# A two-layer SSD, GLA and attention trunk on one core: packed first loads, an earlier norm root, value products beside the next scores, and a rewritten tail

## The chip, the cores and the metric

The kernel runs on one core of a Trainium2 chip. The time is the device time of one execution, in microseconds (us). A core has five engines with a queue of instructions each: PE (TensorE, matrix products; PEld stands for its weight loads), DVE (VectorE), ACT (ScalarE), POOL (GpSimd) and SP (SyncE, which here only starts transfers). Transfers between memory and the core are started from the queue of SP or of ACT.

## What is computed

Sequence 256, width 1024, one batch, fp32. Layer one projects the normed input once and runs an SSD branch (causal convolution, 16 heads) and a GLA branch (8 heads) on parts of it; layer two is an attention whose block is as long as the sequence, so that only the own block, a causal softmax, remains:

```python
def ssd_gla_layer(x, norm_w, w_in, ...):
    h = rms_norm(x, norm_w)
    u = h @ w_in
    z_a, xbc, dt_raw, q_b, k_b, v_b, gate_lr, g_b = split_cols(u, EVEN_SPLITS)
    xbc = silu(causal_depthwise_conv(xbc, conv_w, conv_b))
    y_a = rms_norm(ssd_chunked_scan(...) * silu(z_a), ssd_norm_w)
    log_decay = log_sigmoid(gate_lr @ gate_w2 + gate_b) / 16
    o_b = rms_norm(gla_chunked(q_b, k_b, v_b, log_decay), gla_norm_w) * silu(g_b)
    return x + concatenate([y_a, o_b]) @ w_out

def moba_layer(x, norm_w, w_in, w_out):
    q, k, v, z = split(rms_norm(x, norm_w) @ w_in, 4)   # 16 heads of 64
    o = moba_attention(q, k, v)                         # one block of 256: causal softmax
    return x + (o * silu(z)) @ w_out

reference = lambda x: rms_norm(moba_layer(ssd_gla_layer(x)), final_norm)
```

## The kernel before

Every large product is made in three: both factors are split into a high part (ACT copies, L76) and a low part (DVE subtracts, L77), and PE adds high times high, low times high and high times low (`mm` at L159). In names, `r_` is a raw weight tile, `h_` its high and `l_` its low part. Weights come in chunks over SP's queue (`fetch`, L70) into four buffers, in the order of a list of pieces (`plan`), and are split some chunks ahead (`prefetch`).

PE runs its instructions in exactly the order in which the code writes them. A small model clock decides while the program is written: each product adds its modelled time (`spend`), and steps of coroutines whose delay (table `DL`) is over are written in between the products of the main loop (`spawn`, `step`, `due`). On the other engines a scheduler places the work, but for the first stage, where DVE and ACT too stand in written order.

The stages that the change touches:

- Start. Twenty warm-up products of a zero tile (`warmp`, L177, count `NWARM`). The transposed input `xT` comes in eight chunks (kb) of 128 rows over SP's queue, each followed by the weights of both first column chunks (`a01`, 2 x 416 columns); the constants `cst`, with the norm weights `en` among them, come over ACT's queue (L184). For each chunk the input is scaled by `en` and split (`hh`, L216 to L219), the weights are split (`h_a`, `l_a`), and PE makes twelve products into four banks `pa` (`gemm_a01`). The norm itself is taken out of the products: squares of x are summed to `xsq` (ACT by pairs of chunks at L223, DVE adds), PE sums over rows (`ss`, ahead of chunk 7's products), DVE and POOL make `rcol`, the inverse root (L232, L233), and `tm_evac` scales the banks out with it: `dtr`, `glr` on DVE and `v` on ACT (L266). The next product group, `pb`, takes the first bank that comes free.
- Main list. `ORDER_A` gives the order of column blocks of the input projection: numbers are blocks of 128 columns (convolution input, GLA's queries and keys 14 to 17), "a2" to "a4" are 416-column chunks (value and gate). `GLA_NEEDS` says which of these each GLA part waits for. A block is 24 products, `ks` (L547) is GLA's scaled key.
- Attention. Four groups g of two pairs of heads. For each group the main loop writes the projections `pp` (queries and keys, then gates z), and the coroutine `co_attn` writes scores `as`, the softmax (row maximum as a negated `nm` on DVE at L773, exponent on ACT at L775), transposes `ptp`, and value products `ao` into a bank of the pool `psm`; `og` is ao times the gate, split into `oghi`, `oglo`.
- Tail. The last projection `pf` is made row block by row block (tt = 0, 1); `add_res` adds the residual (L841) and lets ACT sum the squares (L843), `scale_w` multiplies by the final norm's weight `fnb` (L846), `finish` makes the inverse root (L850, L851), scales both halves (ACT L854, DVE L856) and stores them over ACT's and SP's queues. The last 256 columns of tt = 1 have a bank of their own, `pflast`.

## Time and profile before

| what | value |
|---|---|
| device time, median of 3 runs (lowest, highest) | 340.99 us (340.92, 341.36) |
| profiled execution, its own time | 340.65 us |
| its span, first to last instruction | 338.9 us |
| mean granted PE clock | 0.993 |
| busy: PE, PEld, DVE, ACT, POOL | 98%, 87%, 76%, 69%, 9% |
| moved by DMA | 56.06 MB, mean 165 GB/s |

The profile is of one execution. The 1.75 us between its time and its span lie ahead of the first and behind the last instruction. A row of a timeline gives the start, the busy time of a run of like instructions, the engine, the line of code, the operation, output and inputs, their count, and in brackets how long the engine had been idle and what released it. Matmuls overlap in PE's pipeline, so a row's busy time is longer than the step from one product to the next.

### The profile page before, as it was taken

What the parts mean: (1) busy time and instruction counts of PE and PEld (TensorE: products, weight loads), DVE (VectorE), ACT (ScalarE), POOL (GpSimd) and SP (SyncE); (2) the same over time, 40 slices, a digit from 0 to 9 for tenths busy, and PEclk for the clock granted to TensorE, in tenths of its full rate; (3) what the DMA queues carried; (4) which work ended last, traced back from release to release, by engine and by line L of the source; (5) the groups of instructions that cost most, each with busy time, mean ns of one, the idle gap of its engine ahead of it and who ended that gap; (6) DMA issues with size and microseconds to landing.
All of it is one profiled execution on the core that took longest, in us unless ns stands there. A gap on an engine that the chain in (4) does not pass through costs nothing.

```text
span 338.9 us, 5921 instructions
## 1 busy us (share of the span) xinstructions
PE 331.0 (98%) x2160; PEld 295.0 (87%) x2160; DVE 257.1 (76%) x535; ACT 234.8 (69%) x499; POOL 29.7 (9%) x42
## 2 busy tenths in 40 slices
PE   8999999999999999999999999999999999999992
PEld 8999989999899899999888888888888888888791
DVE  3978978999997569789974775467869698696552
ACT  4958699899675758677452676475696887978541
POOL 1000010002100141434210000000000000000000
PEclk9999999999999999999999999999999999999997
DMA  7996784462377454431685635757507346070002
GB/s 227 340 329 198 233 233 134 135 203 91 97 211 263 143 156 158 161 127 55 203 294 192 200 119 179 248 150 240 170 17 254 105 142 232 1 248 3 0 20 106
DMA packets 18093, 56.06 MB, mean 165 GB/s; under 512 B 2048, under 2 KB 5120, under 8 KB 17936
## 3 DMA queue, kind: packets, MB, share of 16 engines
q1 hardware_dynamic: 17344, 53.53, 49.1%
q10 hardware_dynamic: 720, 2.16, 1.8%
q8 instruction: 17, 0.28, 0.3%
q14 instruction: 12, 0.10, 0.1%
HBM read 54.63 MB, written 1.05 MB: 164 GB/s over the span
## 4 chain that ended last, share of the span: by engine, by line
PE 96%; issue 2%; DVE 1%; ACT 0%; POOLq 0%; POOL 0%
PE pb L159 22%; PE pp L159 20%; PE pa L159 14%; PE pc L159 13%; PE pv L159 6%; PE pf L159 5%; PE yp L159 2%; PE ao L159 2%; PE go L159 2%; PE as L159 2%; PE gs L159 2%; PE ptp L163 2%; PE warmp L177 1%; PE obt L163 1%; PE lg L159 1%
## 5 line engine op out<-in xcount | busy, mean ns | idle before, releaser
L159 PE MATMUL pb<-hh,h_b 128*128 128x256 f32 x416 | 76.9, 286 | 0.0
L159 PE MATMUL pp<-h,h_p 128*128 128x512 f32 x192 | 67.7, 403 | 0.0
L159 PEld LDWEIGHTS pb<-hh,h_b 128*128 128x128 f32 x416 | 64.7, 191 | 1.4 <-issue 0.9
L159 PE MATMUL pb<-hh,l_b 128*128 128x256 f32 x208 | 58.8, 282 | 0.0
L159 PE MATMUL pp<-h,l_p 128*128 128x256 f32 x192 | 49.9, 280 | 0.0
L159 PE MATMUL pa<-h_a,hh 128*128 128x416 f32 x160 | 42.9, 360 | 0.0
L159 PEld LDWEIGHTS pp<-h,h_p 128*128 128x128 f32 x192 | 34.5, 188 | 7.0 <-issue 0.5
L159 PEld LDWEIGHTS pb<-hh,l_b 128*128 128x128 f32 x208 | 39.8, 191 | 0.0
L159 PEld LDWEIGHTS pp<-h,l_p 128*128 128x128 f32 x192 | 36.2, 189 | 2.2
L77 DVE TENSOR_TENSOR l_p<-r_p,h_p 128x1024 fp32r<-128x1024 f32 x24 | 29.2, 1223 | 9.2 <-ACT h_p L76 8.3
L77 DVE TENSOR_TENSOR l_b<-r_b,h_b 128x1024 fp32r<-128x1024 f32 x26 | 31.5, 1213 | 3.8 <-ACT h_b L76 3.8
L76 ACT ACTIVATE h_b<-r_b 128x1024 fp32r<-128x1024 f32 x26 | 27.2, 1062 | 9.3 <-DMA r_b<-in_wb 7.0
L159 PEld LDWEIGHTS pa<-h_a,hh 128*128 128x128 f32 x160 | 30.2, 191 | 1.3 <-issue 0.9
L76 ACT ACTIVATE h_p<-r_p 128x1024 fp32r<-128x1024 f32 x24 | 25.2, 1057 | 1.9 <-PE pv L159 1.6
L159 PE MATMUL pa<-l_a,hh 128*128 128x416 f32 x80 | 24.8, 351 | 0.0
L76 ACT ACTIVATE h_c<-r_c 128x1024 fp32r<-128x1024 f32 x16 | 16.9, 1055 | 10.2 <-DMA r_c<-in_wc 7.0
L77 DVE TENSOR_TENSOR l_c<-r_c,h_c 128x1024 fp32r<-128x1024 f32 x16 | 19.9, 1251 | 4.9 <-ACT h_c L76 4.9
L77 DVE TENSOR_TENSOR l_a<-r_a,h_a 128x832 fp32r<-128x832 f32 (+1 forms) x21 | 20.4, 978 | 2.3 <-ACT h_a L76 2.2
L76 ACT ACTIVATE h_a<-r_a 128x832 fp32r<-128x832 f32 (+1 forms) x21 | 18.0, 861 | 4.3 <-DMA r_a<-in_wa 3.1
L159 PE MATMUL pv<-h_v,h 128*128 128x512 f32 x64 | 20.2, 391 | 0.0
L775 ACT ACTIVATE pt<-pt,nm 128x128 f32<-128x128 f32 (+1 forms) x32 | 14.2, 443 | 5.6 <-DVE nm L773 5.6
L446 DVE SCALAR_TENSOR_TENSOR cu<-pad,cwh,cu 128x256 f32<-128x256 f32 x30 | 14.4, 481 | 1.3 <-ACT cu L444 1.2
(235 smaller groups left out, 700.9 us busy)
## 6 DMA issues: line engine op xcount, KB each, us to landing
r_b<-in_wb SPq DMA_DIRECT2D x26, 512.0 KB, 4.4
r_p<-in_wp SPq DMA_DIRECT2D x24, 512.0 KB, 4.2
r_c<-in_wc SPq DMA_DIRECT2D x16, 512.0 KB, 3.9
...
```

The costliest lines, as they stand in the source:

```text
L76: S.activation(hi, raw, AF.Copy)
L77: V.tensor_sub(lo, raw, hi.bitcast(F32))
L159: TE.matmul(out, lhsT, rhs, start=start, stop=stop)
L163: TE.transpose(out, in_, ident)
L177: TE.matmul(wps[:, 0:T], warm[:, 0:P], warm, start=True, stop=True)
L446: V.scalar_tensor_tensor(u, pd[:, 1 + i:1 + i + T], w(i), u, op0=ALU.mult, op1=ALU.add)
L775: S.activation(pt[:, cs], pt[:, cs], AF.Exp, scale=-1.0, bias=nm[:, tt:tt + 1], accum_out=sme[:, tt:tt + 1])
```

## The change

- Loads. A chunk of x^T, its column of norm weights and both weight chunks are packed in one array `xw`, 1092 columns per chunk (559 KB), loaded into shared buffers of the pool `big` and no longer into the four raw buffers. Chunks 0 and 1 come in two transfers: columns 0 to 676 (norm column, x, first weights, 346 KB) over SP's queue and the rest (213 KB) over ACT's; chunk 3 comes over ACT's queue, the others over SP's. `cst` follows on SP's queue. Chunks 6 and 7 use the buffers of 0 and 1 again.
- Fifteen warm-up products for twenty.
- The squares are made chunk by chunk; `ss` and the root `rcol` are written in the middle of chunk 6 and get high priority, as do `rsq` and the evacuation of the four banks. Two small operations on constants move to chunk 5.
- `ORDER_A`: "a3" stands between blocks 2 and 3 (it stood behind block 6), and some blocks behind it change places.
- Value products: for groups 0 to 2 the code of `ao` and `og` is put in a closure `last`, which the next group's coroutine calls ahead of its scores; its bank comes from the pool `psg`. Group 3 runs it behind its transposes. The loop that waited for z is gone.
- Tail: for tt = 1 DVE sums the squares, each sum going on from the last one and starting at D x EPS; `fnb` is multiplied by the root of D once; the root on POOL follows the last sum directly, at high priority; ACT scales and stores columns 0 to 384 and DVE 384 to 1024 (before: halves of 512).

```diff
-NWARM = 20
+XW = 4 + T + 2 * 416
+NWARM = 15
...
-ORDER_A = (8, 9, 10, 11, 0, 14, 1, 12, 2, 13, 3, 15, 5, 16, 4, 17, 6, "a3", 7, "a2", "a4")
+ORDER_A = (8, 9, 10, 11, 0, 14, 1, 12, 2, "a3", 3, 13, 5, 15, 4, 16, 6, 17, 7, "a2", "a4")
...
-    nc.scalar.dma_start(cst, cst_d)
...
+    xTs, ens = [], []
     for kb in range(KB):
-        nc.sync.dma_start(xT[:, kb, :], xT_d[:, kb, :])
-        load(1 if kb else 2)
+        raw = big.tile([P, XW], F32, name=f"xw{kb}", tag=("xT", "y", "gs", "obhi", "oblo", "v", "xT", "y")[kb])
+        for i, (c0, c1) in enumerate(((0, 676), (676, XW)) if kb < 2 else ((0, XW),)):
+            (nc.scalar if i or kb == 3 else nc.sync).dma_start(raw[:, c0:c1], xw_d[:, kb, c0:c1])
+        w = raw[:, 260:XW].rearrange("p (c n) -> p c n", c=2)
+        raws.extend([w[:, 0:1, :], w[:, 1:2, :]] if kb < 2 else [w])
+        ens.append(raw[:, 0:1])
+        xTs.append(raw[:, 4:260])
+    nc.sync.dma_start(cst, cst_d)
...
-    xsq = big.tile([P, KB, T], F32, name="xsq", tag="y")
+    xsq = tmp.tile([P, T], F32, name="xsq0", tag="t1g")
+    cwh = cpool.tile([P, 50], F32, name="cwh")
+    ea = cpool.tile([P, 16], F32, name="ea")
 
     with tc.manual_schedule(engines={mybir.EngineType.DVE, mybir.EngineType.Activation}):
         for kb in range(KB):
-            en = cst[:, C_EN + kb:C_EN + kb + 1]
+            en, xk = ens[kb], xTs[kb]
             if kb == 0:
-                V.tensor_scalar(hhi[:, kb, :], xT[:, kb, :], en, None, op0=ALU.mult)
+                V.tensor_scalar(hhi[:, kb, :], xk, en, None, op0=ALU.mult)
             else:
-                S.activation(hhi[:, kb, :], xT[:, kb, :], AF.Copy, scale=en)
-            V.scalar_tensor_tensor(hlo[:, kb, :], xT[:, kb, :], en, hhi[:, kb, :].bitcast(F32),
+                S.activation(hhi[:, kb, :], xk, AF.Copy, scale=en)
+            V.scalar_tensor_tensor(hlo[:, kb, :], xk, en, hhi[:, kb, :].bitcast(F32),
                                    op0=ALU.mult, op1=ALU.subtract)
-            prefetch(kb + 2)
-            if kb % 2:
-                S.activation(xsq[:, kb - 1:kb + 1, :], xT[:, kb - 1:kb + 1, :], AF.Square)
-                if kb > 1:
-                    V.tensor_tensor(xsq[:, 0:2, :], xsq[:, 0:2, :], xsq[:, kb - 1:kb + 1, :], op=ALU.add)
-        V.tensor_tensor(xsq[:, 0, :], xsq[:, 0, :], xsq[:, 1, :], op=ALU.add)
-        prefetch(10)
+            prefetch((2, 4)[kb] if kb < 2 else kb + 3)
+            sq = tmp.tile([P, T], F32, name=f"xsq{kb}", tag="t1f") if kb else xsq
+            S.activation(sq, xk, AF.Square)
+            if kb:
+                V.tensor_tensor(xsq, xsq, sq, op=ALU.add)
+            if kb == 5:
+                V.tensor_scalar(cwh, cst[:, C_CW:C_CW + 50], 0.5, None, op0=ALU.mult)
+                S.activation(ea, cst[:, C_AL:C_AL + 16], AF.Exp)
+        prefetch(11)
...
-            if kb == 0:
-                w = [tuple(a[:, 0, :] for a in need(("a01", 0, c))) for c in range(2)]
+            if kb < 2:
+                w = [tuple(a[:, 0, :] for a in need(("a01", kb, c))) for c in range(2)]
             else:
-                hi, lo = need(("a01", kb))
+                hi, lo = need(("a01", kb, 0))
                 w = [(hi[:, c, :], lo[:, c, :]) for c in range(2)]
             ts = [slice(tt * P, tt * P + P) for tt in range(2)]
             steps = [[(b, hhi[:, kb, ts[b[1]]], w[b[0]][0]), (b, hlo[:, kb, ts[b[1]]], w[b[0]][0]),
                       (b, hhi[:, kb, ts[b[1]]], w[b[0]][1])] for b in banks]
-            if kb == 0:
+            if kb < 2:
                 order = [t for h in (steps[0:2], steps[2:4]) for q_ in zip(*h) for t in q_]
             elif kb < KB - 1:
                 order = [t for q_ in zip(*steps) for t in q_]
             else:
-                env["rcol"] = rms_from_sum(colsum(xsq[:, 0, :], "ss1")[:, 0:2], 2, D, "rcol")
                 order = [t for q_ in steps for t in q_]
             seen = {}
-            for b, l_, r_ in order:
+            for n, (b, l_, r_) in enumerate(order):
+                if kb == KB - 2 and n == 6:
+                    with tc.high_priority():
+                        env["rcol"] = rms_from_sum(colsum(xsq, "ss1")[:, 0:2], 2, D, "rcol")
                 seen[b] = i = seen.get(b, -1) + 1
                 mm(ps[b][:, 0:416], l_, r_, kb == 0 and i == 0, kb == KB - 1 and i == 2)
...
+        with tc.high_priority():
+            V.tensor_tensor(rsq, rcol, rcol, op=ALU.mult)
+            for c in range(2):
+                for tt in range(2):
+                    tm_evac(c, tt, ps[c][tt])
...
+        if "ao" in env:
+            env.pop("ao")()
...
+            if pr == prs[0]:
+                yield DL["at1"]
+        def last():
+            ops = pg(f"ao{g}")
+            for n, pr in enumerate(prs):
+                hc = [slice(64 * (2 * pr + j), 64 * (2 * pr + j) + 64) for j in range(2)]
+                for j, r in enumerate(rows):
+                    mm(ops[r, n * T:n * T + T], va[:, 0, hc[j]], pTs[pr, j][:, 0:T], True, False)
+                for j, r in enumerate(rows):
+                    mm(ops[r, n * T + P:n * T + T], va[:, 1, hc[j]], pTs[pr, j][:, T:3 * P], False, True)
+            for n, pr in enumerate(prs):
+                og = tmp.tile([P, T], F32, name=f"og{pr}", tag="t1f")
+                V.tensor_tensor(og, ops[:, n * T:n * T + T], env[("z", pr)], op=ALU.mult)
+                S.activation(oghi[:, pr, :], og, AF.Copy)
+                V.tensor_sub(oglo[:, pr, :], og, oghi[:, pr, :].bitcast(F32))
+        if g < 3:
+            env["ao"] = last
+        else:
+            yield DL["at3"]
+            last()
...
+        if tt == 0:
+            S.activation(jk[:, 0:c1 - c0], x1[:, tt, cs], AF.Square, accum_out=ssf[:, tt, i:i + 1])
+        else:
+            V.tensor_tensor_reduce(out=jk[:, 0:c1 - c0], in0=x1[:, tt, cs], in1=x1[:, tt, cs], scale=1.0,
+                                   scalar=ssf[:, tt, i - 1:i] if i else D * EPS, op0=ALU.mult, op1=ALU.add,
+                                   accum_out=ssf[:, tt, i:i + 1])
...
+    V.tensor_scalar(fnb, fnb, D ** 0.5, None, op0=ALU.mult)
+    def root(tt, s):
+        rv = sm.tile([P, 1], F32, name=f"rv{tt}", tag="rv")
+        G.tensor_tensor(rv, s, mhalf[:, 0:1], op=ALU.pow)
+        return rv
+    def finish(tt, r):
         o = big.tile([P, D], F32, name=f"o{tt}", tag=f"s{tt}")
-        S.activation(o[:, 0:512], x1[:, tt, 0:512], AF.Copy, scale=r)
-        nc.scalar.dma_start(out_d[tt * P:tt * P + P, 0:512], o[:, 0:512])
-        V.tensor_scalar(o[:, 512:D], x1[:, tt, 512:D], r, None, op0=ALU.mult)
-        nc.sync.dma_start(out_d[tt * P:tt * P + P, 512:D], o[:, 512:D])
+        c = 384
+        S.activation(o[:, 0:c], x1[:, tt, 0:c], AF.Copy, scale=r)
+        nc.scalar.dma_start(out_d[tt * P:tt * P + P, 0:c], o[:, 0:c])
+        V.tensor_scalar(o[:, c:D], x1[:, tt, c:D], r, None, op0=ALU.mult)
+        nc.sync.dma_start(out_d[tt * P:tt * P + P, c:D], o[:, c:D])
...
+            if i == 1:
+                r = root(1, ssf[:, 1, 2:3])
         scale_w(512 + 256 * i, 768 + 256 * i, 1)
-        if i == 0:
-            V.tensor_tensor(sf[:, 1:2], ssf[:, 1, 0:1], ssf[:, 1, 1:2], op=ALU.add)
-            V.tensor_scalar(sf[:, 1:2], sf[:, 1:2], 1.0 / D, EPS, op0=ALU.mult, op1=ALU.add)
-    finish(1, sf[:, 1:2], ssf[:, 1, 2:3])
+    finish(1, r)
```

SP's queue at the start. Before, the list begins with:

```order
L190 DMA xT<-in_xT 128x256
L70 DMA r_a_0_0_113<-in_wa 128x416
L70 DMA r_a_0_1_115<-in_wa 128x416
L190 DMA xT<-in_xT 128x256
L70 DMA r_a_1_118<-in_wa 128x2x416
L190 DMA xT<-in_xT 128x256
L70 DMA r_a_2_121<-in_wa 128x2x416
```

The same queue after:

```order
L194 DMA xw_105<-in_xw 128x676
L194 DMA xw_108<-in_xw 128x676
L194 DMA xw_111<-in_xw 128x1092
L194 DMA xw_115<-in_xw 128x1092
L194 DMA xw_117<-in_xw 128x1092
L194 DMA xw_119<-in_xw 128x1092
L194 DMA xw_121<-in_xw 128x1092
L199 DMA cst<-in_cst 128x111
```

Seventeen transfers of x and weights became seven here and three on ACT's queue, and `cst` came over from ACT's queue to the end.

PE in the attention layer, where the value products of group 2 stand (`pp_1`, `pp_2` are projections of group 3, `as` its scores). Before:

```order
L159 MATMUL pp_1_3614<-h_2307,h_p_3496 128x512
L159 MATMUL pp_1_3614<-h_2307,l_p_3497 128x256
L159 MATMUL ao_3623<-pT_3535,va 64x256 x2
L159 MATMUL ao_3623<-pT_3535,va 64x128 x2
L159 MATMUL ao_3623<-pT_3586,va 64x256 x2
L159 MATMUL ao_3623<-pT_3586,va 64x128 x2
L159 MATMUL pp_1_3614<-h_2307,h_p_3496 128x512
L159 MATMUL pp_1_3614<-h_2307,l_p_3497 128x256
```

After:

```order
L159 MATMUL pp_2_3681<-h_2311,h_p_3573 128x512
L159 MATMUL pp_2_3681<-h_2311,l_p_3574 128x256
L159 MATMUL ao_3686<-pT_3539,va 64x256 x2
L159 MATMUL ao_3686<-pT_3539,va 64x128 x2
L159 MATMUL ao_3686<-pT_3590,va 64x256 x2
L159 MATMUL ao_3686<-pT_3590,va 64x128 x2
L159 MATMUL as_0_3703<-qk_1_3565,pp_0_s 128x128
L159 MATMUL as_1_3705<-qk_1_3565,pp_0_s 128x128
```

The value products moved from between key projections to directly ahead of the scores of group 3, some thirty rows further on.

DVE at the end, from the last-but-one addition of the residual on. Before:

```order
L841 TENSOR_TENSOR x_1662<-x_1662,pf_1_3782 128x256
L846 TENSOR_TENSOR x_1662<-x_1662,fnb 128x256
L885 TENSOR_TENSOR sf<-ssf 128x1
L886 TENSOR_SCALAR sf<-sf 128x1
L841 TENSOR_TENSOR x_1662<-x_1662,pflast 128x256
L846 TENSOR_TENSOR x_1662<-x_1662,fnb 128x256
L850 TENSOR_SCALAR rv_4005<-ssf,sf 128x1
L856 TENSOR_SCALAR o_4008<-x_1662,rv_4005 128x512
```

After (`ISA` is the reducing operation and the read of its sum):

```order
L862 TENSOR_TENSOR x_1666<-x_1666,pf_1_3787 128x256
L867 ISA jf_3976,ssf<-x_1666,ssf 128x256
L867 ISA ssf 128x1
L872 TENSOR_TENSOR x_1666<-x_1666,fnb 128x256
L862 TENSOR_TENSOR x_1666<-x_1666,pflast 128x256
L867 ISA jf_4004,ssf<-x_1666,ssf 128x256
L867 ISA ssf 128x1
L872 TENSOR_TENSOR x_1666<-x_1666,fnb 128x256
L888 TENSOR_SCALAR o_4009<-x_1666,rv_4006 128x640
```

The sums of squares came to DVE, its small additions went, and the last scaling grew from 512 to 640 columns.

## Rows read from the trace of the kernel before

**Rows 1.** Page, busy times; windows view of the tail: PE, PEld, DVE, ACT, POOL, clock.
```profile
PE 331.0 (98%) x2160; PEld 295.0 (87%) x2160; DVE 257.1 (76%) x535; ACT 234.8 (69%) x499; POOL 29.7 (9%) x42
...
325.20:338.90 13.70, 7.08 (x54) 6.64 (x53) 6.38 (x16) 4.01 (x12) 1.10 (x2) 0.83 0.20 78
```

**Rows 2.** Timeline of the first microseconds: start, busy us, engine, line, operation.
```profile
1.25 4.34 PEld L177 LDWEIGHTS warmp<-warm 128*128 128x128 f32 x20 [1.25 <-DVE mhalf L203]
...
4.42 1.11 ACT L76 ACTIVATE h_a<-r_a 128x416 fp32r<-128x416 f32 x2 [0.24 <-DMA r_a<-in_wa]
...
5.69 1.36 PE L159 MATMUL pa<-h_a,hh 128*128 128x416 f32 x4
...
7.27 0.91 PE L159 MATMUL pa<-h_a,hh 128*128 128x416 f32 x4
```

**Rows 3.** Timeline of PE alone from 6.3 on.
```profile
6.04 1.01 PE L159 MATMUL pa<-h_a,hh 128*128 128x416 f32 x3
```

**Rows 4.** Windows of the loading; last columns: granted clock, DMA share, GB/s.
```profile
2.00:3.00 1.00, 1.00 (x7) 1.00 (x6) 0.00 (x0) 0.53 (x1) 0.13 (x4) 1.00 0.79 173
3.00:4.00 1.00, 1.00 (x7) 1.00 (x7) 0.03 (x1) 0.03 (x1) 0.00 (x0) 1.00 0.99 347
```

**Rows 5.** Tile r_a in the first 20 us: durations ns min/median/max, first and last start.
```profile
L76 ACT ACTIVATE h_a<-r_a x9: 550/883/902, 4.4 to 17.1; 128x832 fp32r<-128x832 f32 x7, 128x416 fp32r<-128x416 f32 x2
L77 DVE TENSOR_TENSOR l_a<-r_a,h_a x9: 591/1018/1026, 5.0 to 18.1; 128x832 fp32r<-128x832 f32 x7, 128x416 fp32r<-128x416 f32 x2
```

**Rows 6.** Timeline around the first root.
```profile
21.98 0.50 PE L159 MATMUL ss<-ones,xsq 128*128 128x1 f32 x4
...
22.76 0.70 POOL L233 TENSOR_TENSOR rcol<-rcol_v,mhalf 128x2 f32<-128x2 f32 x1 [20.63 <-DVE rcol_v L232]
...
24.24 1.55 ACT L266 ACTIVATE v<-pa,rsq 128x384 f32<-128x384 f32 x3 [1.19 <-DVE glr L263]
...
24.52 0.34 PE L159 MATMUL pa<-l_a,hh 128*128 128x416 f32 x1
24.88 0.30 PEld L159 LDWEIGHTS pb<-hh,h_b 128*128 128x128 f32 x2 [0.35 <-ACT v L266]
```

**Rows 7.** Timeline of PE at the value products of group 2.
```profile
274.98 0.40 PE L159 MATMUL pp<-h,h_p 128*128 128x512 f32 x1
275.22 0.28 PE L159 MATMUL pp<-h,l_p 128*128 128x256 f32 x1
275.43 1.52 PE L159 MATMUL ao<-pT,va 128*64 128x256 f32 x16
276.88 0.50 PE L159 MATMUL pp<-h,h_p 128*128 128x512 f32 x1
277.21 0.28 PE L159 MATMUL pp<-h,l_p 128*128 128x256 f32 x1
```

**Rows 8.** Timeline at the start of group 3's softmax.
```profile
285.10 0.48 DVE L773 CUSTOM_DVE_ANT_0 pt<-as,mat,rq 128x256 f32<-128x256 f32 x1
285.27 0.40 ACT L775 ACTIVATE pt<-pt,nm 128x128 f32<-128x128 f32 x1 [1.38 <-DVE nm L773]
```

**Rows 9.** Timeline of GLA's scaled key on POOL and its first products.
```profile
84.66 1.21 POOL L547 COPY ks<-e 128x256 f32<-128x256 f32 x1 [3.52 <-DVE e L538]
...
111.67 0.37 PE L159 MATMUL gs<-qs,ks 64*128 64x128 f32 x1
```

**Rows 10.** Timeline of the tail.
```profile
332.32 0.42 DVE L841 TENSOR_TENSOR x<-x,pflast 128x256 f32<-128x256 f32 x1 [1.19 <-PE pflast L159]
...
333.94 0.55 POOL L851 TENSOR_TENSOR rv<-rv,mhalf 128x1 f32<-128x1 f32 x1 [5.33 <-DVE rv L850]
334.53 0.72 ACT L854 ACTIVATE o<-x,rv 128x512 f32<-128x512 f32 x1 [1.25 <-POOL rv L851]
...
335.05 0.34 SPq L857 DMA_DIRECT2D out<-o  x1
335.28 0.35 ACTq L855 DMA_DIRECT2D out<-o  x1
```

More of the change, by code (lines that the diff above doesn't have):

```diff
@@ L101, in plan_tm @@
             plan((name, q_), src[:, 2 * q_:2 * q_ + 2, :], 2, src.shape[2])
[L103 to L106 removed]
+    for kb in range(KB):
+        for c in range(2 if kb < 2 else 1):
+            plan(("a01", kb, c), None, 1 if kb < 2 else 2, 416)
     for j in ORDER_A:
         if isinstance(j, str):
[L109 removed]
+            plan_tm(j, wa_d[int(j[1]) - 2])
         else:
@@ L361, in co_first @@
         rcol = env["rcol"]
+        with tc.high_priority():
[3 more added lines that the diff above has]
+                    tm_evac(c, tt, ps[c][tt])
         V.tensor_scalar(rhalf, rcol, 0.5, None, op0=ALU.mult)
-        V.tensor_tensor(rsq, rcol, rcol, op=ALU.mult)
         V.tensor_scalar(rsv, rsq, 1.0 / P, None, op0=ALU.mult)
         V.tensor_scalar(rsh, rsq, 0.5, None, op0=ALU.mult)
-        V.tensor_scalar(cwh, cst[:, C_CW:C_CW + 50], 0.5, None, op0=ALU.mult)
-        S.activation(ea, cst[:, C_AL:C_AL + 16], AF.Exp)
-        for c in range(2):
-            for tt in range(2):
-                tm_evac(c, tt, ps[c][tt])
         env["a1"] = True
@@ L788, in co_attn @@
                 S.activation(pTs[pr, j], tp[:, 0:3 * P], AF.Copy)
-            yield DL["at1"] if pr == prs[0] else DL["at3"]
-        ops = pm(f"ao{g}")
-        for n, pr in enumerate(prs):
-            hc = [slice(64 * (2 * pr + j), 64 * (2 * pr + j) + 64) for j in range(2)]
-            for j, r in enumerate(rows):
-                mm(ops[r, n * T:n * T + T], va[:, 0, hc[j]], pTs[pr, j][:, 0:T], True, False)
-            for j, r in enumerate(rows):
-                mm(ops[r, n * T + P:n * T + T], va[:, 1, hc[j]], pTs[pr, j][:, T:3 * P], False, True)
-        while ("z", prs[1]) not in env:
-            yield 300
-        for n, pr in enumerate(prs):
-            og = tmp.tile([P, T], F32, name=f"og{pr}", tag="t1f")
-            V.tensor_tensor(og, ops[:, n * T:n * T + T], env[("z", pr)], op=ALU.mult)
-            S.activation(oghi[:, pr, :], og, AF.Copy)
-            V.tensor_sub(oglo[:, pr, :], og, oghi[:, pr, :].bitcast(F32))
+            if pr == prs[0]:
[18 more added lines that the diff above has]
+            last()
     for g in range(4):
@@ L869, in trunk @@
         scale_w(512 * n, 512 * n + 512, 0)
-    V.tensor_scalar(sf[:, 0:1], ssf[:, 0, 0:1], 1.0 / D, EPS, op0=ALU.mult, op1=ALU.add)
-    finish(0, sf[:, 0:1], ssf[:, 0, 1:2])
+    V.tensor_scalar(sf[:, 0:1], ssf[:, 0, 0:1], ssf[:, 0, 1:2], D * EPS, op0=ALU.add, op1=ALU.add)
+    finish(0, root(0, sf[:, 0:1]))
     part(pf[0, 1], "f0", oghi, oglo, 1, rest, ("f0", 3))
@@ L904, in _pack @@
     cst = np.zeros((P, C_N), f)
-    cst[:, C_EN:C_EN + 8] = col(a["even_norm"][0])
     cst[:, C_SN:C_SN + 8] = col(a["even_ssd_norm"][0])
@@ L942, in _pack @@
     }
-_ORDER = ["xT", "x", "cst", "mat", "gw2", "fn", "wa", "wb", "wc", "wv", "wp", "wf"]
+_ORDER = ["xw", "x", "cst", "mat", "gw2", "fn", "wa", "wb", "wc", "wv", "wp", "wf"]
 def kernel(**inputs):
```

33 lines of the change are left out of this document (12 added, 21 removed).

## The prediction, made before the result was known

> **What bounds the kernel now.** I read the page's busy times first: PE is busy for 331.0 us, 98% of the span [rows 1], and its instructions stand in a written order, so only time in which PE has no useful work can be won. PE's rows show three such places and some joints. At the start PE runs twenty warm-up products, and its first real product starts at 5.69 [rows 2]. The three products from 6.04 on take 1.01 us, of which the last has 0.35: they start 0.33 to 0.35 apart [rows 3]. The four from 7.27 take 0.91, so 0.19 apart [rows 2]. These are 416 columns at 1.2 GHz and at 2.4 GHz: three products (5.69, 6.04, 6.38) ran at the lower level and the rise came at about 6.7, though the granted clock reads 1.00 ahead of it too [rows 4]. In the middle, the weight load of the first `pb` product waits 0.35 us for `v` [rows 6]. At the end, the add at 332.32 waits for PE's last product, and behind it the chain of add, squares, root, scaling and store fills the rest of the span [rows 10]. The profiled execution took 340.65 us; the median of the runs is 340.99, so 0.34 is added to a result on the profile's scale.
>
> **Start: packed loads on two queues, fifteen warm-ups.** The twenty warm-up weight loads take 4.34 us from 1.25 on, 0.217 each [rows 2]; fifteen end at 1.25 + 15 x 0.217 = 4.5. Before, the warm-ups came last: the first `h_a` started at 4.42 and takes 0.55 [rows 2, 5], so it was there at 4.97, and PE took it up at 5.69. With five warm-ups fewer the load decides, and the question is when the first piece (346 KB: x, its norm column and the first weights) lands. It is the first transfer on SP's queue; ACT's starts 213 KB and 213 KB beside it. From the rates 173 and 347 GB/s in the two windows [rows 4], 520 KB pass between 2.0 and 4.0. If the queues share equally, 2 x 346 = 692 KB have passed when the piece is there: 4.0 + (692 - 520)/347 = 4.5. I take 4.6, as some bytes behind a piece pass before its completion is seen. Early end: larger rows reach 347 GB/s from 2.0 on, 2.0 + 692/347 = 4.0, and less if SP's piece is served ahead of the other: 3.8. Late end: now the `h_a` at 4.42 had 396 KB ahead of it or beside it (60 of `cst`, 128 of x, 208 of weights); 692 is 296 more, 0.85 at 347: 5.3. Then `h_a` 0.55 and a weight load 0.2: first product at 5.35 (4.55 to 6.05), with PE idle from 4.5 for 0.85.
> If the rise stays at 6.7, being 0.34 us early is one more product at the lower level, worth 0.19 at the higher: **0.2 us** (0.6 won at 4.55, 0.2 lost at 6.05). Where the idle stretch moves the rise, that is rival A.
> Feeding afterwards: a chunk costs ACT at most 0.55 (hh, fewer columns than the smaller `h_a`) + 0.90 (`h_a`) + 0.55 (Square, likewise) = 2.0 us and DVE 0.48 (hlo, by the 256-wide operation) + 1.02 (`l_a`) + 0.42 (add) = 1.92 [rows 5, 8, 10]; PE takes 12 x 0.19 = 2.28, so squares by the chunk stay hidden. `cst` goes to SP's end, but nothing needs it ahead of chunk 5. Chunks 6 and 7 reuse the buffers of 0 and 1, whose readers are done by then. These cost nothing.
> One rule speaks against the second queue; the sum can do without it. The Trainium skill ("DMA: Bandwidth & Descriptors", section "Issuing engines are not separate DMA queues") says that transfers started by several engines run on the same 16 DMA engines and interleave, so that a second issuer saves issue time only. The trace agrees so far that 347 GB/s came with one queue loaded; by the rule the piece lands at 4.5 or later, and without it, alone on the engines, it would be there by 3.8, and 0.6 would stand for 0.2 in the sum.
>
> **Urgent root.** The column sum moves from ahead of chunk 7 (21.98) to the middle of chunk 6. Its POOL root started at 22.76 for 0.70, and `v`, behind some small DVE operations, at 24.24, 1.55/3 = 0.52 each [rows 6]. Six products earlier is 6 x 0.19 = 1.1: the root is over by 22.4. The first bank is complete nine products (three banks of three) before the end, 24.52 - 1.7 = 22.8. With rsq first and only dtr and glr (16 columns each, together less than one `v`) beside it, `v` ends by 23.9. `pb` can start at 24.52 + 0.19 = 24.71 instead of 24.88, so the wait goes: 0.17 at least, the whole 0.35 at most, **0.25** taken. The cover is 0.8 us. The sum itself now needs xsq by 21.98 - 1.1 - 0.2 = 20.7; the last `l_a` starts at 18.1 [rows 5], and behind its 1.02 one add of 0.42 is over at 19.6. Should the squares come over a microsecond later, PE waits for them instead and the 0.25 is gone.
>
> **Chunk a3 moved up, blocks reordered.** The keys' blocks come later by a3 (48 products x 0.19 = 9.1 us) and about two blocks of 24 x 0.12 = 2.9: 15 us. Now `ks` is over at 84.66 + 1.21 = 85.9 and first used at 111.67 [rows 9], 25 us of slack. Worth nothing; PE does the same products.
>
> **Value products ahead of the next scores.** In a run of `pp`, an `l_p` product of 256 columns follows 0.24 us after an `h_p` of 512 (274.98 to 275.22), so 256 columns take 0.12. But `ao` starts 0.21 after the `l_p`, and the second `pp` behind ao 0.33 after the first (276.88 to 277.21) [rows 7]: 0.09 lost at each joint. With `ao` next to `as`, two of four joints fall away, 0.18 in each of groups 0 to 2, 0.54. The joint from ao to as is in no row; it lies between 0 and 0.18. I take **0.35** (0 to 0.55), near the middle. What `ao` reads has been ready for longer than now. On DVE two og products come to stand ahead of the softmax's first row maximum and two oglo behind it. It is late already: ACT sat idle for 1.38 until DVE's nm at 285.27 [rows 8]. The work is only moved, so I take nothing; rival C prices it.
>
> **Tail.** Now the add starts at 332.32 (0.42), the root at 333.94 (0.55), the scaling at 334.53, the issues come at 335.05 on SP and 335.28 on ACT [rows 10]; between add and root lie ACT's squares and a DVE operation. After, the squares are summed on DVE: nearest row the 256-wide reducing operation, 0.48 [rows 8]. Add until 332.74, sum until 333.22, 0.05 to POOL (as from root to scaling), root until 333.82, scaling at 333.87: 0.66 early. ACT's 384 columns instead of 512 take some 0.15 less, DVE's 640 some 0.1 more: issues at about 334.5 on both, 0.78 early on ACT and 0.55 on SP, with 512 KB to store as before. **0.7** (0.4 if SP's 320 KB end last, 0.85). scale_w stands beside POOL's root, whose 0.55 covers its 0.43 or so. The one pass that multiplies fnb (1024 columns, 1.25 by `l_a`'s 1.02 for 832) can go anywhere ahead: nothing.
>
> **Sum**: 0.2 + 0.25 + 0.35 + 0.7 = 1.5 us. 340.65 - 1.5 = 339.15, and with the 0.34: **339.5**.
>
> **The rivals.**
> A: the idle stretch after fifteen warm-ups puts off the rise to 2.4 GHz. For it: in the last 13.7 us, in whose second half PE stood idle, the mean granted clock is 0.83 [rows 1], so idling does bring the lower level back; against it: that idle time is 6.6 us, this one 0.85. If chunk 0 and a third of chunk 1 (16 products) run at the lower level instead of 3, 13 x (0.345 - 0.19) = 2.0 is lost and 0.34 won: 340.65 + 1.67 - 1.3 = 341.0, on the median's scale 341.3, no change. Beside this row stands the Trainium skill's "TensorE: Matmul & The Clock Gate", section "What's actually happening": the throttled state is the default, and activity releases it. Taken strictly, the rule makes fewer warm-ups with a gap behind them this rival; no row here shows so short a gap.
> B, the one that ends slower: the first piece lands at 5.3 because the queues share; PE is idle from 4.5 to 6.05, and the lower level holds for all 24 products of chunks 0 and 1. Lost: 0.36 at the start and 21 x 0.155 = 3.2; 340.65 + 3.6 - 1.3 = 342.95, or 343.3. It decides from a loss of 2.0 at the start (the 1.3 and 0.7 beyond). For it: half the rate for the first piece; against: 4.42 for the present first weights.
> C: the og products delay the softmax by about 0.65, and PE waits for the transposes in two groups: 339.5 + 1.3 = 340.8. Against: `pp` products stand between, as now.
> D: the change doesn't do what it says: the joints stay (0) and the 640 columns end last (0.4): 340.65 - 0.2 - 0.25 - 0.4 = 339.8, or 340.1.
>
> **How the numbers follow.** Forecast 0.62, A 0.13, B 0.10, C 0.08, D 0.07. A measurement of this kernel can tell about 0.2%, 0.68 us, from no change: faster is below 340.3, slower above 341.7. Faster: the forecast but for its weakest terms, and most of D, 0.66. Slower: B and the upper part of A, 0.12. Same: the rest, 0.22. With every term at its better end (0.6, 0.35, 0.55, 0.85) the time would be 338.64; I take 338.5. The high end reaches over A's middle, 341.3; B stays out.
>
> **What the profile after would show.** Right: first `pa` at 5.2 to 5.5, and products 0.19 apart from 6.7 on; no PE wait between the last `pa` and `pb`; `as` right behind `ao`, without a wait; the last scaling 1.55 us behind the last add. Wrong: products 0.35 apart beyond 7.5 (A, B); weight loads of `ptp` that wait for ACT (C); `as` 0.2 behind ao, or SP's store landing last by over 0.3 us (D).

## The result, and the profile after

The changed kernel took 342.72 us (median of 4 runs, 342.69 to 344.11) where the kernel before took 340.96 in the same session: a ratio of 1.0061, with a 95% interval of 1.0047 to 1.0075. It is 1.8 us slower, outside the range given, and on the other side of zero.

The profiled execution is the one of 344.11, some 1.4 above the other three; why is told below, with rival A. By the page's busy times PE is busy for 1.2 us more than before and idle for 2.2 more [rows 1]:

```profile
PE 332.2 (97%) x2155; PEld 296.0 (86%) x2155; DVE 258.3 (75%) x542; ACT 232.0 (68%) x498; POOL 27.9 (8%) x42
```

To see where the time went I read the start of the same PE products in each trace. The columns: the first `pa`, the first `pb`, from there to the first `pp` (all of layer one behind the first stage), from there to the first `pf`, the end of `pflast`, and from there to the end of the span. The last three rows are experiments that are told further on.

| profile of | first pa | first pb | pb to pp | pp to pf | PE's end | behind it |
|---|---|---|---|---|---|---|
| before | 5.69 | 24.88 | 199.49 | 82.56 | 332.28 | 6.66 |
| after | 5.43 | 26.47 | 201.14 | 82.74 | 335.66 | 6.65 |
| a_obfirst (after, one edit without effect) | 5.28 | 25.32 | 201.22 | 82.52 | 334.35 | 6.64 |
| u_order (after, old order) | 5.40 | 26.42 | 199.44 | 82.54 | 333.71 | 6.66 |
| best | 4.62 | 24.28 | 199.39 | 82.51 | 331.46 | 6.97 |

So none of the terms of the sum arrived: the start lost 0.4 to 1.6 where 0.45 was to be won, layer one lost 1.7 where nothing was to happen, attention is even, and so is the tail. The start has to be read with care: in the five other profiles with the old start (b_order, b_attn, b_aomid, b_tail, t_stt) the first `pb` comes at 24.66 to 25.50, so that 0.4 is no more than executions differ by. By the runs, u_order, which has all of the change but the order, lies 0.1 above the kernel before.

**Start.** The timeline of the changed kernel (start, busy us, engine, line, operation) answers to [rows 2]:

```profile
4.83 0.99 ACT L77 ACTIVATE h_a<-xw 128x416 fp32r<-128x416 f32 x2 [1.32 <-DMA xw<-in_xw]
...
5.43 1.76 PE L159 MATMUL pa<-h_a,hh 128*128 128x416 f32 x4 [0.61 <-ACT h_a L77]
...
9.76 1.29 PE L159 MATMUL pa<-h_a,hh 128*128 128x416 f32 x4
...
11.27 0.91 PE L159 MATMUL pa<-h_a,hh 128*128 128x416 f32 x4
```

The first piece is there at 4.83 (4.6 was expected), the first product starts at 5.43, and PE stood idle for 0.61. The products from 9.76 on are still 0.31 apart on average ((1.29 - 0.35)/3), those from 11.27 on 0.19: in this execution PE ran at 1.2 GHz until about 10.6, where before it rose at 6.7 [rows 3]. That is rival A, and it happened in this run.

**First root.** DVE and POOL in the same profile, in place of [rows 6]:

```profile
19.97 2.35 DVE L78 TENSOR_TENSOR l_b<-r_b,h_b 128x1024 fp32r<-128x1024 f32 x2
23.18 0.16 DVE L244 TENSOR_SCALAR rcol_v<-ss 128x2 f32<-128x2 f32 x1 [0.86 <-PE ss L159]
...
23.40 1.22 DVE L78 TENSOR_TENSOR l_b<-r_b,h_b 128x1024 fp32r<-128x1024 f32 x1
```

```profile
23.42 1.76 POOL L245 TENSOR_TENSOR rcol<-rcol_v,mhalf 128x2 f32<-128x2 f32 x1 [21.29 <-DVE rcol_v L244]
```

The root, marked urgent, takes 1.76 us instead of 0.70. A weight split of 1.22 us starts on DVE just ahead of it, and it ends 0.56 after the split. In this execution nothing waits for it: PE, still late from its lower clock, starts the last `pa` at 26.28 and the first `pb` right behind it. Where the clock rose early, PE does wait; that profile stands below, with u_hold.

**Layer one.** DVE ahead of the last transposes of GLA, then PE, in the kernel before:

```profile
147.74 1.21 DVE L77 TENSOR_TENSOR l_c<-r_c,h_c 128x1024 fp32r<-128x1024 f32 x1
...
150.00 1.12 DVE L597 SCALAR_TENSOR_TENSOR ob<-go,rr,gs 128x128 f32<-128x128 f32 x4
```

```profile
150.87 0.74 PE L163 MATMUL obt<-mat,ob 128*128 128x128 f32 x4
```

And in the changed one:

```profile
150.18 1.21 DVE L78 TENSOR_TENSOR l_c<-r_c,h_c 128x1024 fp32r<-128x1024 f32 x1
...
152.44 1.21 DVE L78 TENSOR_TENSOR l_c<-r_c,h_c 128x1024 fp32r<-128x1024 f32 x1
153.57 1.12 DVE L608 SCALAR_TENSOR_TENSOR ob<-go,rr,gs 128x128 f32<-128x128 f32 x4
```

```profile
154.23 0.96 PE L163 MATMUL obt<-mat,ob 128*128 128x128 f32 x4 [1.10 <-DVE ob L608]
```

PE waits 1.10 us for `ob`, which, counted from the transposes of the pair before, stands behind two splits on DVE where it stood behind one. A second new wait is that of `gs` for an exponent on ACT:

```profile
112.55 0.37 PE L159 MATMUL gs<-e,e 64*128 64x128 f32 x1 [0.29 <-ACT e L500]
```

**Attention**, the value products of the second group and the scores of the third, which answer to [rows 7] (the rows call these groups 2 and 3; in the code, which counts from 0, they are 1 and 2):

```profile
284.15 0.82 PE L159 MATMUL ao<-pT,va 128*64 128x256 f32 x8
...
284.90 0.49 PE L159 MATMUL as<-qk,pp_s 64*128 64x128 f32 x4
...
285.76 0.41 DVE L842 TENSOR_TENSOR qkl<-qk,qkh 128x256 fp32r<-128x256 f32 x1
...
286.23 0.39 PE L159 MATMUL as<-qkl,qkh 64*128 64x256 f32 x2
```

The scores do follow ao directly, but the products that read `qkl` start only when DVE has made it, 0.5 us behind the ones ahead of them.

**Tail**, which answers to [rows 10]:

```profile
335.70 0.42 DVE L862 TENSOR_TENSOR x<-x,pflast 128x256 f32<-128x256 f32 x1 [0.82 <-PE pflast L159]
...
336.69 0.42 DVE L872 TENSOR_TENSOR x<-x,fnb 128x256 f32<-128x256 f32 x1
336.73 0.79 POOL L880 TENSOR_TENSOR rv<-ssf,mhalf 128x1 f32<-128x1 f32 x1 [4.36 <-DVE ssf L867]
337.55 0.61 ACT L886 ACTIVATE o<-x,rv 128x384 f32<-128x384 f32 x1 [4.53 <-POOL rv L880]
...
338.14 0.34 SPq L889 DMA_DIRECT2D out<-o  x1
338.20 0.36 ACTq L887 DMA_DIRECT2D out<-o  x1
```

From add to scaling it is 1.85 us instead of 2.21, and from add to the last issue 2.50 instead of 2.96. The root again runs beside a DVE pass, and takes 0.79 instead of 0.55.

### The profile page after: what moved, and what is told of

Same layout as the page of the kernel before. It is cut to its first block, busy times and chain, and to the rows that moved or that the text cites. A ratio compares the mean times of both kernels' runs of the same rounds, so it can differ in the third digit from the quotient of the medians.

```text
span 342.3 us, 5904 instructions
## 1 busy us (share of the span) xinstructions
PE 332.2 (97%) x2155; PEld 296.0 (86%) x2155; DVE 258.3 (75%) x542; ACT 232.0 (68%) x498; POOL 27.9 (8%) x42
## 4 chain that ended last, share of the span: by engine, by line
PE 93%; DVE 2%; issue 1%; DMA 1%; ACT 1%; POOL 0%; POOLq 0%
PE pb L159 22%; PE pp L159 20%; PE pa L159 14%; PE pc L159 13%; PE pv L159 6%; PE pf L159 5%; PE yp L159 2%; PE go L159 2%; PE ptp L163 2%; PE gs L159 1%; PE as L159 1%; PE ao L159 1%; DMA xw<-in_xw 1%; PE lg L159 1%; PE ab L159 1%
## 5 line engine op out<-in xcount | busy, mean ns | idle before, releaser
L159 PE MATMUL pa<-h_a,hh 128*128 128x416 f32 x160 | 44.5, 369 | 0.6 <-ACT h_a L77 0.6
L159 PEld LDWEIGHTS pa<-h_a,hh 128*128 128x128 f32 x160 | 31.4, 198 | 2.1 <-ACT h_a L77 0.9
L159 PE MATMUL pa<-l_a,hh 128*128 128x416 f32 x80 | 25.7, 361 | 0.0
L159 PEld LDWEIGHTS pa<-l_a,hh 128*128 128x128 f32 x80 | 15.6, 195 | 0.2
L77 ACT ACTIVATE h_a<-r_a 128x832 fp32r<-128x832 f32 x12 | 10.8, 900 | 6.6 <-PE pb L159 6.6
```

The lines of the kernel that those rows point to most:

```text
L77: S.activation(hi, raw, AF.Copy)
L159: TE.matmul(out, lhsT, rhs, start=start, stop=stop)
```

## The experiments

Each was compared with the kernel before, run beside it on the same chip (medians 341.03, 340.90, 340.94 and 340.94 in the four sessions). Names with u_, a_ and h_, and best, start from the changed kernel, those with b_ and t_ from the kernel before. Each session was on another chip, so medians of two sessions are compared below only with this in mind.

### The order of blocks

u_order puts the old list into the changed kernel; b_order puts the new list into the kernel before, the same two lines the other way round:

```diff
-ORDER_A = (8, 9, 10, 11, 0, 14, 1, 12, 2, "a3", 3, 13, 5, 15, 4, 16, 6, 17, 7, "a2", "a4")
+ORDER_A = (8, 9, 10, 11, 0, 14, 1, 12, 2, 13, 3, 15, 5, 16, 4, 17, 6, "a3", 7, "a2", "a4")
```

> The changed kernel with the old ORDER_A. In the changed kernel's profile PE waits 1.26 us longer than before for the last GLA transposes (obt waits for ob on DVE, where the split l_c stands ahead of it now) and 0.5 us for gs. Theory 1 (the new order of blocks makes these waits): they go, 342.7 - 1.8 = 340.9. Rival (they come from the new start, the loads or the root, which shift DVE): they stay, 342.7.

> The kernel before with nothing but the new ORDER_A. Theory 1: the two waits appear here too, 341.0 + 1.8 = 342.8, with PE idle 1.2 to 1.4 us ahead of the last obt. Rival: no wait there, 341.0 as before.

u_order: 341.16 us (12 runs), ratio 0.9993 (0.9981 to 1.0006). b_order: 342.90 (6 runs), 1.0045 (1.0032 to 1.0059). The order alone takes 1.9 us by the medians, 1.5 by the ratio and 1.7 in the stretch from pb to pp (201.22 against 199.49), and without it the changed kernel is as fast as the one before. b_order's trace has the wait at the same place, with the old start, attention and tail around it:

```profile
151.54 1.21 DVE L77 TENSOR_TENSOR l_c<-r_c,h_c 128x1024 fp32r<-128x1024 f32 x1
...
152.67 1.12 DVE L597 SCALAR_TENSOR_TENSOR ob<-go,rr,gs 128x128 f32<-128x128 f32 x4
...
153.33 0.95 PE L163 MATMUL obt<-mat,ob 128*128 128x128 f32 x4 [1.09 <-DVE ob L597]
```

a_obfirst tried to bring ob forward by priority, a_obbuf by buffers of its own for every second pair of heads:

```diff
-            for tt in range(2):
-                V.scalar_tensor_tensor(ob[:, tt * P:tt * P + P], op[:, tt * P:tt * P + P], rr[:, tt:tt + 1],
-                                       gs[:, tt, vc], op0=ALU.mult, op1=ALU.mult)
+            with tc.high_priority():
+                for tt in range(2):
+                    V.scalar_tensor_tensor(ob[:, tt * P:tt * P + P], op[:, tt * P:tt * P + P], rr[:, tt:tt + 1],
+                                           gs[:, tt, vc], op0=ALU.mult, op1=ALU.mult)
```

```diff
-            ob = tmp.tile([P, T], F32, name=f"ob{h}", tag="t1f")
+            ob = tmp.tile([P, T], F32, name=f"ob{h}", tag=("t1f", "obx")[b % 2])
```

> The changed kernel, new order kept, with only the products ob given high priority on DVE. Theory 1a (the place of ob behind a weight split in DVE's queue is what PE waits for): 1.2 us less, 341.5. Rival 1b (GLA's own chain comes too late because its blocks do, wherever ob stands on DVE): 342.7.

> The changed kernel, new order kept, with a second pair of buffers for ob, so that ob of heads 6 and 7 no longer waits for the transposes of heads 4 and 5 and stands ahead of the weight splits on DVE (a_obfirst did not move it). Theory 1a: the wait of 1.26 us ahead of the last obt goes, 342.7 - 1.3 = 341.4. Rival 1b (GLA's chain is late in itself): 342.7.

a_obfirst: 342.74 (6 runs), 1.0051 (1.0034 to 1.0068). The edit changed nothing in the place of ob: the split stands ahead of it as before, so the run says nothing on the theory. It served in another way: its profile shows the changed start with an early clock. a_obbuf: 341.46 (12 runs), 1.0006 (0.9993 to 1.0019), 1.3 below the changed kernel, as theory 1a had it:

```profile
148.50 1.11 DVE L608 SCALAR_TENSOR_TENSOR ob<-go,rr,gs 128x128 f32<-128x128 f32 x4
...
149.87 1.21 DVE L78 TENSOR_TENSOR l_c<-r_c,h_c 128x1024 fp32r<-128x1024 f32 x1
...
152.39 0.60 PE L163 MATMUL obt<-mat,ob 128*128 128x128 f32 x4
```

ob starts 3.9 us ahead of its transposes instead of right in front of them. It had waited for a buffer: two buffers hold ob, and those of heads 6 and 7 could be written only when the transposes of heads 4 and 5 had read theirs; in that gap the scheduler had put two splits on DVE, with the old order one. With the buffers, the stretch from pb to pp is 199.53, that of before, in the new order.

### The first root

u_hold (from u_order) makes the low parts of the second and third block with an operation that reads a one computed from the root, so that they can't run ahead of it (the pieces 11 and 12 of the list; in this stage splits are also made fewer pieces ahead):

```diff
         S.activation(hi, raw, AF.Copy)
-        V.tensor_sub(lo, raw, hi.bitcast(F32))
+        if len(got) in (11, 12):
+            V.scalar_tensor_tensor(lo, raw, held["one"], hi.bitcast(F32), op0=ALU.mult, op1=ALU.subtract)
+        else:
+            V.tensor_sub(lo, raw, hi.bitcast(F32))
...
+                        held["one"] = cpool.tile([P, 1], F32, name="one1")
+                        V.tensor_scalar(held["one"], env["rcol"][:, 0:1], 0.0, 1.0, op0=ALU.mult, op1=ALU.add)
```

> The changed kernel with the old ORDER_A, and with the low parts of the second and third weight block (l_b) made by an operation that also reads a one computed from rcol, so that DVE can't run them ahead of or beside the first root. In the profile of a_obfirst, where PE's clock rose early, POOL's root took 1.76 us beside such a DVE pass (0.70 before) and PE waited 1.17 for v. Theory (DVE's passes ahead of and beside the root delay it): the root takes 0.7 again, PE's wait goes, about 1.0 below u_order: 340.2. Rival (the start is bound by the loads or by ACT, or the root is slow for itself): as u_order, 341.2.

340.58 (12 runs), 0.9992 (0.9974 to 1.0011), 0.6 below u_order by the medians as they stand. First the root in a_obfirst, where the clock was early and PE came to the end of `pa` sooner:

```profile
22.33 1.21 DVE L78 TENSOR_TENSOR l_b<-r_b,h_b 128x1024 fp32r<-128x1024 f32 x1
22.35 1.76 POOL L245 TENSOR_TENSOR rcol<-rcol_v,mhalf 128x2 f32<-128x2 f32 x1 [20.22 <-DVE rcol_v L244]
...
24.15 0.35 PE L159 MATMUL pa<-l_a,hh 128*128 128x416 f32 x1
...
25.32 0.51 PE L159 MATMUL pb<-hh,h_b 128*128 128x256 f32 x2 [0.81 <-ACT v L278]
```

And in u_hold:

```profile
21.48 0.70 POOL L249 TENSOR_TENSOR rcol<-rcol_v,mhalf 128x2 f32<-128x2 f32 x1 [19.35 <-DVE rcol_v L248]
...
22.57 1.28 DVE L79 SCALAR_TENSOR_TENSOR l_b<-r_b,one,h_b 128x1024 fp32r<-128x1024 f32 x1
23.76 0.23 DVE L278 SCALAR_TENSOR_TENSOR dtr<-pa,rcol,cst 128x16 f32<-128x16 f32 x1
...
24.86 0.51 PE L163 MATMUL pb<-hh,h_b 128*128 128x256 f32 x2 [0.24 <-ACT v L282]
```

With no pass beside it the root takes 0.70 again and is over 1.9 us earlier, and PE's wait shrinks from 0.81 to 0.24. What is left comes from the next thing in DVE's queue: one split stands ahead of dtr. The first `pb` comes 0.46 earlier. The medians give 0.45, if each is taken against the kernel before of its own session (341.03 and 340.90): about half of the 0.9 to 1.0 expected. The intervals of the two ratios overlap, so the gain rests on the traces; and the run has two edits, the held splits and the fewer pieces ahead, which it can't part.

### The loads and the warm-ups

h_onequeue and h_warm20 (both from u_hold):

```diff
-            (nc.scalar if i or kb == 3 else nc.sync).dma_start(raw[:, c0:c1], xw_d[:, kb, c0:c1])
+            nc.sync.dma_start(raw[:, c0:c1], xw_d[:, kb, c0:c1])
```

```diff
-NWARM = 15
+NWARM = 20
```

> u_hold with all first loads on SP's queue, in the same order. Theory (the two queues share the rate, so the first piece waits for bytes that are needed later): the first piece lands by about 4.2 instead of 4.8, the first pa starts 0.3 to 0.6 us earlier than 5.13 to 5.43, and the time is 0.1 to 0.3 below u_hold's 340.6. Rival (a second queue adds rate or saves issue time on SP): the later pieces land later, PE waits between chunks 0 to 3, and the time is 0.3 or more over u_hold's.

> u_hold with twenty warm-up products again. So far some 10 of 46 timed runs with fifteen lie 1 to 2 us above the others of the same kernel (342.2 to 342.6 for u_hold), and 7 of about 100 with twenty; the profiles with a late rise to 2.4 GHz (9.4 to 10.6) are all with fifteen. Theory (the idle stretch of 0.3 to 0.6 us behind fifteen makes the rise late in some runs, and costs nothing in the others): the median is 0.1 to 0.3 over u_hold's 340.6 because the first pa waits for warm-ups until 5.7, and no run lies 1.4 over it. Rival (the late rise has nothing to do with the count): the same median or better, and two or three of twelve runs at 342.3.

h_onequeue: 340.21 (12 runs), 0.9982 (0.9973 to 0.9990). One queue is 0.4 faster than two by the medians; these are of two sessions, and the intervals overlap:

```profile
3.77 1.06 ACT L77 ACTIVATE h_a<-xw 128x416 fp32r<-128x416 f32 x2 [1.69 <-DMA xw<-in_xw]
...
4.62 1.07 PE L163 MATMUL pa<-h_a,hh 128*128 128x416 f32 x4
```

The first piece is there at 3.77 instead of 4.52 in u_hold (4.83 in the changed kernel), and fifteen warm-ups then end right ahead of the first product. The Trainium skill ("DMA: Bandwidth & Descriptors", section "Issuing engines are not separate DMA queues") has transfers of several issuers interleave on the same engines; these landings agree with it. The first `pb` comes 0.54 earlier than in u_hold (24.32 against 24.86), but in the profiled execution a product `lg` that waits for DVE takes 0.37 of that back.

h_warm20: 340.48 (11 runs), 0.9987 (0.9978 to 0.9995), 0.1 below u_hold where 0.1 to 0.3 above it was expected. The first product starts at 5.50, later by 0.4, and it costs nothing, since PE is held up at the third chunk anyway. The first product of that chunk in u_hold, then in h_warm20:

```profile
10.28 1.77 PE L163 MATMUL pa<-h_a,hh 128*128 128x416 f32 x8 [0.18 <-ACT h_a L77]
```

```profile
10.03 1.70 PE L163 MATMUL pa<-h_a,hh 128*128 128x416 f32 x8
```

In u_hold PE waits there for `h_a`, since ACT could start on the chunk only when it had landed, at 8.93; the 0.4 won at the first product is gone by then. In h_onequeue PE waits 0.40 at the same place. No run of h_warm20 lies high: the highest is 340.86, while three of u_hold's twelve are at 342.24 to 342.59. That fits the theory, but it doesn't show it: the kernel before, with twenty warm-ups, has six of 58 runs at 342.07 to 342.97 in the first two sessions, and none of 29 above 341.48 in the session of h_warm20.

### Attention and tail, each alone

b_attn and b_tail put only the attention part and only the tail into the kernel before. b_aomid writes ao between the scores of both pairs. t_stt is b_tail without the pass beside the last root, and with 512 columns for ACT:

```diff
-        if "ao" in env:
-            env.pop("ao")()
         sps = {}
         for pr, (qt, kt) in zip(prs, qks):
+            if pr == prs[1] and "ao" in env:
+                env.pop("ao")()
```

```diff
-        scale_w(512 + 256 * i, 768 + 256 * i, 1)
+        if i == 0:
+            scale_w(512 + 256 * i, 768 + 256 * i, 1)
...
+        if tt:
+            V.scalar_tensor_tensor(o[:, e:D], x1[:, tt, e:D], r, fnb[:, e:D], op0=ALU.mult, op1=ALU.mult)
```

> The kernel before with only the attention part (value products directly ahead of the next scores). In the changed kernel's profile two joints per group fell away (0.18 x 3 = 0.55) and the scores waited 0.41 and 0.24 us for qkl on DVE. Theory: the wait belongs to this part, so alone it nearly cancels itself: 341.0 (340.8 to 341.2). Rival: the wait comes from the later stages' shift in the changed kernel; alone it saves 0.55: 340.4.

> The kernel before with the attention part, the value products placed between the scores of the two pairs of heads instead of ahead of both. In b_attn the scores of the second pair waited 0.3 to 0.4 us for qkl in one group. Theory (the joints are worth 0.18 per group and the wait for qkl takes most of it back): one more joint of 0.09 per group, but no wait: 340.9 - 0.3 + 0.27 - 0.4, so 340.5 to 340.7 against 341.0. Rival (the value products cost the softmax more than the joints give): 341.0 or more.

> The kernel before with only the new tail. In the changed kernel's profile the way from the last add to the landed store is 5.14 us against 5.38, since the root takes 0.79 instead of 0.55 and both stores start together and share the rate. Theory: 0.25 less than before, 340.8. Rival (the prediction's sum; the landing in that one profile was an outlier): 0.7 less, 340.3.

> b_tail with no DVE pass beside the last root: the last 256 columns are multiplied by root and fnb in one operation behind it, and ACT takes 512 columns. Theory (a DVE pass beside POOL's root stretches it): the root takes 0.55 instead of 0.79, the scalings take 0.15 longer, the time is within 0.15 of b_tail. Rival (the root's length has nothing to do with DVE): the root stays at 0.8 and the time is 0.15 to 0.2 over b_tail.

b_attn: 340.91 (12 runs), 0.9994 (0.9986 to 1.0003). b_aomid: 340.89 (12 runs), 1.0004 (0.9994 to 1.0013). Neither is told from no change. In b_attn the wait for qkl is there without the other parts:

```profile
282.78 0.37 PE L159 MATMUL as<-qkh,qkh 64*128 64x256 f32 x2
283.28 0.39 PE L159 MATMUL as<-qkl,qkh 64*128 64x256 f32 x2
```

0.50 from one to the next, where the first pair's take 0.20. On DVE `qkl` stands behind a weight split:

```profile
281.68 1.22 DVE L77 TENSOR_TENSOR l_p<-r_p,h_p 128x1024 fp32r<-128x1024 f32 x1
282.81 0.42 DVE L831 TENSOR_TENSOR qkl<-qk,qkh 128x256 fp32r<-128x256 f32 x1
```

In the kernel before it was done at 282.65, and its products started at 283.02. The stretch from pp to pf is 82.54 in b_attn and 82.53 in b_aomid, 82.56 before. In b_attn the steps from product to product add up: two joints fewer in each of three groups give 0.58, and the products that come late or start anew behind `qkl` take 0.51. In b_aomid that wait is gone, and so is the gain: ao has a step of 0.21 on either side there, as it had between projections, and the scores behind it begin with another of 0.21, so the joints are as many as before.

b_tail: 340.74 (12 runs), 0.9988 (0.9976 to 1.0001), 0.16 less, near the 0.25 expected and far from 0.7; the interval still holds no change. t_stt: 340.69 (12 runs), 0.9991 (0.9977 to 1.0006), the same as b_tail. The last root in b_tail and then in t_stt:

```profile
333.93 0.43 DVE L851 TENSOR_TENSOR x<-x,fnb 128x256 f32<-128x256 f32 x1
333.97 0.79 POOL L859 TENSOR_TENSOR rv<-ssf,mhalf 128x1 f32<-128x1 f32 x1 [4.36 <-DVE ssf L846]
```

```profile
333.15 0.55 POOL L859 TENSOR_TENSOR rv<-ssf,mhalf 128x1 f32<-128x1 f32 x1 [4.36 <-DVE ssf L846]
```

0.79 beside the pass and 0.55 without it, as the theory said. The longer scaling took 0.14 of the 0.24 back (the last issue comes 2.43 us behind PE's end, 2.53 in b_tail), and the larger store on ACT's queue the rest.

### What beats both

best joins what held: old order, packed loads on one queue, fifteen warm-ups, early column sum, the held splits moved behind dtr and glr as well, attention as changed, and the tail of t_stt. Its edit against h_onequeue, beside that tail:

```diff
-                        V.tensor_scalar(held["one"], env["rcol"][:, 0:1], 0.0, 1.0, op0=ALU.mult, op1=ALU.add)
...
+            V.tensor_scalar(held["one"], glr[:, 1, 0:1], 0.0, 1.0, op0=ALU.mult, op1=ALU.add)
```

> h_onequeue with the held splits moved behind the small evacuations dtr and glr too (in h_onequeue and u_hold PE still waited 0.5 to 0.6 us for v there, since one l_b stood ahead of dtr), and with the tail of t_stt. Theory (DVE's order around the first root is what bounds the start): PE's wait ahead of the first pb shrinks to 0.1, and the time falls by 0.3 to 0.4 below h_onequeue's 340.2, to 339.8. Rival (the held splits are then missing at the second and third block): the wait moves to pb's second block, 340.2 or more.

339.82 us (5 runs, 339.62 to 340.25), ratio 0.9963 (0.9949 to 0.9977): 1.1 below the kernel before and 2.9 below the changed one.

```profile
21.49 0.70 POOL L249 TENSOR_TENSOR rcol<-rcol_v,mhalf 128x2 f32<-128x2 f32 x1 [19.36 <-DVE sel L418]
...
23.49 0.23 DVE L279 TENSOR_SCALAR glr<-pa,rcol 128x16 f32<-128x16 f32 x1
...
24.07 2.48 DVE L79 SCALAR_TENSOR_TENSOR l_b<-r_b,one,h_b 128x1024 fp32r<-128x1024 f32 x2
...
24.28 0.40 PE L163 MATMUL pb<-hh,h_b 128*128 128x256 f32 x2
```

The first `pb` has no wait, at 24.28 against 24.88 before: it comes 0.18 behind the last `pa` (24.10), where it was 0.47 in h_onequeue (23.85 to 24.32). The third chunk landed later in this execution, so that `pb` itself is only 0.04 earlier than there. best has two edits against h_onequeue, the held splits and the tail; the run doesn't say how the 0.4 parts between them.

## Why the prediction was wrong

**The order, taken as nothing, is nearly the whole slowdown** (+1.9 us alone, 1.8 measured). Of the 3.2 us between 339.5 and 342.7 it is over half; the rest is the four terms of the sum that did not arrive. The step that failed is the sentence on the slack of `ks`. Its 25 us were real, and nothing waits for ks. But a moved chunk moves everything behind it against everything else, and I followed one tile. The chain further on, go to ob to obt, had no slack: two buffers tie ob of one pair to the transposes of the pair before, and DVE, which that sentence left out, is an ordered queue in which one more split came to stand ahead. That rival, a later link of GLA's chain, was not among mine, and the chance for slower stood on another mechanism (B), which did not occur.

**The start, 0.45 with the root, lost 0.4 instead** by the profile with an early clock (25.32 against 24.88), and 0.1 by the runs. The landing (4.6, measured 4.67 and 4.83) and the first product (5.35, measured 5.28 to 5.43) came near the forecast. What failed is the root: "over by 22.4" left out that DVE runs splits ahead of `rcol_v` and beside the root; it was over at 24.11. The column sum came early, and waited. With an early clock PE was done with pa at 24.3 (24.15 and a step of 0.19), 0.4 earlier than before, so that the 0.2 of the loads did arrive; but it stood until 25.32, and there it was swallowed. A second step was put at nothing and isn't: "these cost nothing", of the feeding, counts what ACT and DVE do for a chunk, and not when the third chunk lands. PE waits for it in u_hold and h_onequeue, so that a first product that is earlier by fewer warm-ups alone wins nothing, as h_warm20 shows. And the second queue cost what I had priced it at: the first piece was there at 3.77 on one queue, at the early end that I gave (3.8).

**Rival A was right in kind and wrong as an outcome.** By the spacing of pa the rise came late, at 9.4 to 10.6, in the profiles of after, u_order and a_obbuf (PE idle for 0.56 to 0.61 behind the warm-ups), and not in a_obfirst (0.45) and u_hold (0.3). At the first pb the late rise makes 1.15 us, 26.47 against 25.32. But three of four runs of the changed kernel lie at 342.7, as does the profiled one of a_obfirst (342.80), so its median doesn't hold it. The Trainium skill ("TensorE: Matmul & The Clock Gate", section "What's actually happening") has activity release the throttle, which goes with this; what decides in one execution wasn't settled here.

**Attention, 0.35, gave 0.** The joints were sized rightly: two of them fall away per group, 0.19 together where 0.18 was forecast. The place that I took as safe was the other side: the scores come no later than before, and `qkl`, which had 0.4 us to spare, comes behind a weight split on DVE. C named the wrong operand (the softmax; it was qkl).

**The tail, 0.7, gave 0.2 alone and nothing in sum.** The sums on DVE took what was forecast. Two steps failed: the root has no cover for scale_w but is stretched by it (0.79 for 0.55), so that of the 0.55 and 0.78 by which the issues were to come earlier (SP's and ACT's) 0.29 and 0.46 were left; and the stores take longer. Before, SP's was issued 0.23 ahead of ACT's; now both start together, and they take longer, from issue to landing (KB, us):

```profile
out<-o SPq DMA_DIRECT2D x1, 320.0 KB, 2.5
out<-o ACTq DMA_DIRECT2D x1, 192.0 KB, 2.6
```

Before it was 2.1 and 2.4 for 256 KB each. By the transfers in the traces, the last byte is stored 4.83 us behind PE's end, where it was 5.07: that 0.24 arrived. But behind the last byte the span goes on for 1.82 us, where it was 1.59. In best the stores are issued 2.4 us behind PE's end instead of 3.0, yet the span goes on for 6.97: they took 3.3 and 2.8 there, and the span ends 2.14 behind the last byte. One thing goes with these differences. The same view of the changed kernel has a packet on a queue for instructions:

```profile
q14 instruction: 1, 0.01, 0.7%
```

Such a packet stands behind the last stores' issue in all eight profiles of the changed kernel and of those made from it, and in none of the six others. With it the span goes on for 1.82 to 2.14 us behind the last byte, without it for 1.58 to 1.73; b_tail and t_stt, the new tail without it, end 6.40 and 6.44 behind PE's end. So the 0.2 that the tail won alone may have gone to this packet; no run took it away, and the cause stays open.
